# A 4096 x 4096 matmul by two levels of seven products: three first products in quarters, stores by row tile pairs, two more column pairs with kept sums

## The chip, the cores and the metric

The kernel runs on one core of one Trainium2 chip. The metric is the device time of one execution in microseconds. Three executions of the kernel before took 1523.41, 1525.5 and 1526.43 us, so the median is 1525.5 us.

A core has TensorE (PE, with its weight loads PEld), VectorE (DVE), ScalarE (ACT), GpSimd (POOL) and SyncE (SP). SP, ACT and POOL also issue transfers; each of the three has a queue of its own to the 16 DMA engines of the core.

## The reference

```python
def reference(a, b, alpha):          # a, b: 4096 x 4096 float32, alpha: 0.01
    x = np.matmul(a, b)
    return np.where(x > 0, x, alpha * x)
```

## The kernel before, in words

**Tiles.** The output is cut into regions of 1024 x 1024. Row groups g and column pairs j both run from 0 to 3. Region (0, 0) is done directly; the other fifteen stand in the list `regions` in this order: (0,1) (0,2) (0,3), then (1,2) (1,0) (1,3) (1,1), then (2,2) (2,0) (2,3) (2,1), then (3,2) (3,0) (3,1) (3,3). For a region, A is four blocks of 512 x 2048 (A11, A12, A21, A22) and B four blocks of 2048 x 512 (B11, B12, B21, B22), all in fp16 in SBUF. A block of B is two tiles (k = 0, 1) of 128 x 8 x 512.

**Outer level.** The eight block products are replaced by seven (`PRODUCTS`), over sums of A blocks (S1 to S4) and of B blocks (T1 to T4) that DVE makes: product 0 is A11 B11, product 1 is A12 B21, product 2 is S2 T2, product 3 is S3 T3, product 4 is S1 T1, product 5 is A22 T4 and product 6 is S4 B22. The T sums are made in place: T3 in the tiles of B12 and T2 in those of B11. In full, a product is 64 matmuls of 128 x 128 x 512 (line L831, `product`), into four PSUM banks, one for each row tile.

**Inner level.** Some products are themselves done by the same scheme, "in quarters": seven quarter products (`quarter_product`, L770) of 16 matmuls of 128 x 128 x 256, so 112 half-width matmuls in place of 64 full ones. Their operands are again sums: of quarters of a B block (`t3_of_b`, `sums_of_b`, on DVE) and of quarters of an A operand (`sums_of_a`). The sums of A are made once in the first region of a row group (those of S1 in the second), stored to DRAM (`kept_q`) and loaded again in each region by `load_sums` (L762), 512 KB each. In the kernel before, a region of groups 1 to 3 that is neither the first nor the last of its group, and (3,3), does products 3, 4, 5 and 6 in quarters (fourth, fifth, sixth and seventh in the code) and products 0, 1 and 2 in full. The first region of a group does its last two products in quarters; the last region of groups 1 and 2, which also brings in the next group's A ("turning"), does one.

**Order.** `manual_schedule` keeps each engine's instructions in the order in which the program writes them, and each engine works in that order. SP's queue thus holds, from the sixth product of a region to the start of the next region: stores of the V pair of outputs (`leave(v_pairs, 1, 1)`), loads of the next region's B21 (`fetch_b(i + 1, [(1, 0)])`, L544 where they come from `kept_half`), stores of the U2 pair (`leave(u2_pairs, 1, 0)`), then, behind the seventh product, loads of the next B22, the first half of S2 (`load_s2`, L789), and the stores of the last pair. ACT's queue carries the four sums for the seventh product. POOL's queue brings B from the input with a cast from fp32 (L547), two transfers of 512 KB for each tile.

**Buffers.** Three tiles of 16 KB a partition (`x_pool`) hold S1, S4 and, by turns, S2 and a tile `t` of four quarter sums. Three quarter-sized tiles (`a16_pool`) hold further sums and the rooms of the measures. Two output tiles for each of two sides (`c_pool`) are shared by U1, U2, V and the last pair; a tile is free again when its store has landed. `bank` sets alternate between regions: Y and Z are four PSUM banks each.

**Measures.** Every block of A and B is squared once on ACT (L231) and its column or row sums folded on DVE (L240 to L264) for a test of the input's range. Where a block is measured stands in `EARLY` and `MEASURED`.

**Kept data.** For column pair 2, T3 and T2 are stored in group 1 and loaded in groups 2 and 3 (`move_t`, L529). For pairs 0, 1 and 3 B21 and B22 are kept in fp16 (`kept_half`).

The two lines by which a PSUM bank of a first product becomes the start of the next sums (L1132) and a pair of outputs is stored (L1076) are

```python
        for mt in range(MT):
            nc.scalar.copy(z[mt], y[mt])
...
                for m in range(2):
                    nc.sync.dma_start(place(g, h, 2 * r + m, j, nt), t[:, m, :])
```

Of the kernel before, what the change touches and what calls it, by code (L numbers as in the profile page):

```python
# [37 lines left out]
OTHERS = (0, 3)  # L38

# [9 lines left out]
def kernel(  # L49
# [145 lines left out]
    def place(g, h, mt, j, nt):  # L195
        row = ((g * 2 + h) * MT + mt) * P
        col = (j * 2 + nt) * NT
        return out[row:row + P, col:col + NT]

# [314 lines left out]
    kept_t = {name: dram_pool.tile([2, P, KC * NT], DT, name=f"kept_{name}") for name in ("t3", "t2")}  # L514
# [12 lines left out]
    def move_t(name, t, k, out, queue=nc.sync):  # L527
        ends = kept_t[name][k], t.rearrange("p c n -> p (c n)")
        queue.dma_start(*(ends if out else ends[::-1]))  # L529

    def fetch_unit(i, u, nt, later=False):
# [7 lines left out]
        if g > 1 and j == CACHED and (half, nt) == (0, 1):  # L539
            move_t("t3", t, u, False)  # L540
# [89 lines left out]
    def judge(line):  # L630
# [29 lines left out]
        (1, 3): [B11], (2, 0): [B21], (2, 3): [B21], (2, 1): [B12], (3, 1): [B11, B21],  # L660
# [14 lines left out]
    kept_q = {name: dram_pool.tile([4, P, QUARTER], DT, name=f"kept_q{name}") for name in ("a22", "s4", "s1")}  # L675
    FIFTH = {(1, 0), (1, 3), (2, 0), (2, 3), (3, 0), (3, 1), (3, 3)}
# [123 lines left out]
    in_quarters = False  # L800
    for i, (g, j) in enumerate(regions):
# [6 lines left out]
        ybank = 0 if i % 2 == 0 else 4  # L808
        zbank = 4 - ybank
# [6 lines left out]
        def product(n, banks, first):  # L816
            name, half, nt = PRODUCTS[n]

# [3 lines left out]
            if n == 0 or n == 2 and in_fourth:  # L822
                order[-16:] = [(mt, k, c) for mt in range(MT) for k, c in todo[-4:]]
            elif n == 1 or n == 4 and in_fourth:
                order[:16] = [(mt, k, c) for mt in range(MT) for k, c in todo[:4]]
# [14 lines left out]

        def keep(banks, side):
            pairs, kept = new_c(side)
            for mt in range(MT):
                nc.scalar.copy(kept[mt], banks[mt])  # L844
            return pairs, kept

# [51 lines left out]
        def fifth_in_quarters(y, banks, tq, sx, pairs, between):  # L898
# [6 lines left out]
            onto = lambda r, n: [y[2 * r + m][:, n * HALF:(n + 1) * HALF] for m in range(2)]  # L905
# [6 lines left out]
            def more(r, n, room):  # L912
                for m, to in enumerate(onto(r, n)):
                    nc.vector.tensor_add(to, to, room[:, m])

            quarter_product(x[0, 1], b[1, 0], onto(0, 0))
            quarter_product(x[0, 0], b[0, 0], into(chain), True)
            one = copied(0, 0, chain)
            quarter_product(a_quarter(sx[4]), b[1, 1], onto(0, 1))
# [3 lines left out]
            quarter_product(x[1, 1], t(4), onto(1, 0))  # L923
# [9 lines left out]
            last = copied(1, 1, chain)  # L933
            for m in range(2):
# [3 lines left out]
        def sixth_in_quarters(pairs, banks, v_pairs, v, y, tq, sq):  # L938
# [20 lines left out]
            add(v, y)  # L959
# [28 lines left out]
        def seventh_in_quarters(y, one, other, tq, sq):  # L988
# [7 lines left out]
            onto = lambda r, n: [y[2 * r + m][:, n * HALF:(n + 1) * HALF] for m in range(2)]  # L996
            quarter_product(x[0, 1], b[1, 0], onto(0, 0))
# [3 lines left out]
            quarter_product(x[1, 1], t(4), onto(1, 0))  # L1001
# [8 lines left out]
            for mt in range(MT):  # L1010
                nc.vector.tensor_add(kept[mt], y[mt], kept[mt])
            return pairs

        def seventh_at_the_end(y, one, other, tq, sq, one_more):
# [9 lines left out]
            onto = lambda r, n: [part(y[2 * r + m], n) for m in range(2)]  # L1024
# [8 lines left out]
            for mt in (2, 3):  # L1033
                nc.scalar.copy(part(kept[mt], 1), part(y[mt], 1))
            quarter_product(x[0, 1], b[1, 0], onto(0, 0))
            for mt in range(2):
                more(mt, 0, part(y[mt], 0))
# [7 lines left out]
            quarter_product(sx(4), b[1, 1], onto(0, 1))  # L1045
            for mt in range(2):
                more(mt, 1, part(y[mt], 1))
# [7 lines left out]
            quarter_product(x[1, 1], t(4), onto(1, 0), by_row=True)  # L1055
            for mt in (2, 3):
                more(mt, 0, part(y[mt], 0))
# [12 lines left out]
        def leave(pairs, h, nt, some=(0, 1)):  # L1070
            for r, t in enumerate(pairs):
# [3 lines left out]
                for m in range(2):  # L1075
                    nc.sync.dma_start(place(g, h, 2 * r + m, j, nt), t[:, m, :])  # L1076
# [34 lines left out]
        y = [new_bank(ybank + mt) for mt in range(MT)]  # L1111
        z = [new_bank(zbank + mt) for mt in range(MT)]
# [6 lines left out]
        in_fifth = (g, j) in FIFTH  # L1119
        second_of_group = in_fourth and regions[i - 2][0] != g  # L1120
        early = [measure(i, *block) for block in EARLY.get((g, j), [])]
        for m in early[:1]:
# [3 lines left out]
        product(0, y, True)  # L1126
        if second_of_group:
            sums_of_s3(g, (2,))
        for m in early[:1]:
            m.end()  # L1130
        for mt in range(MT):
            nc.scalar.copy(z[mt], y[mt])  # L1132
        if second_of_group and g in [of for of, _ in FIFTH]:
            sums_of_a(g, "s1", new_a16)
        for m in early[1:]:
            m.begin()
        have_t2 = g > 1 and j == CACHED
        if have_t2:
            for k in ks:
                t = have_b[i, k, 0] = b_pool.tile([P, KC, NT], DT, name="b", tag="b11")  # L1140
                move_t("t2", t, k, False, nc.scalar)
        if middle:
            middle.begin()
        for k in ks:
            if have_t2:
                break
# [9 lines left out]
        for m in early[1:]:  # L1156
# [6 lines left out]
        note_rows()  # L1163
        if first_of_group:
# [35 lines left out]
        if in_fifth:  # L1200
# [8 lines left out]
        if in_fifth:  # L1209
# [265 lines left out]
```

## Time and profile before

| | before |
|---|---|
| median of three executions | 1525.5 us |
| profiled execution, its own time | 1526.13 us |
| its span, first to last instruction | 1524.2 us |
| mean granted TensorE clock | 0.999 |
| PE busy | 1512.9 us (99%) |
| DVE busy | 1166.7 us (77%) |
| ACT busy | 512.2 us (34%) |
| POOL busy | 258.3 us (17%) |
| DMA, mean over the span | 244 GB/s |
| moved on SP's queue | 232.95 MB |
| moved on POOL's queue | 112.22 MB |
| moved on ACT's queue | 25.56 MB |

Busy PE is a modelled number: matmuls are pipelined, so a share of 99% says that PE hardly waited, not that each matmul ran at its peak. Times in the views are microseconds from the start of the span. "L831" is line 831 of the kernel. A row of the engines' timeline is a start, a duration to the last end, and a group of like instructions; in square brackets stands how long the engine was idle ahead of it and what it then waited for. A row of DMA issues gives the queue, the count, the size of one transfer and the median time from its issue to its landing.

### The profile page before, as it was taken

The numbers are of one execution on the slowest core, as the hardware profiler recorded it, in microseconds if no ns is written. First come the engines' busy times: TensorE is split into PE (matmuls) and PEld (weight loads), VectorE is DVE, ScalarE is ACT, GpSimd is POOL, SyncE is SP. The second block draws the span as 40 slices with busy tenths as digits, with TensorE's granted clock in tenths as the row PEclk, the third lists the DMA queues.
The fourth block names the chain that finished last, engine by engine and source line by source line (L and its number), as shares of the span: only waits on it lengthen the run. The fifth ranks groups of instructions, "written<-read, shape, count | busy, mean of one in ns | idle before, by whom it ended". The sixth has DMA issues, their size and how long they took to land.

```text
span 1524.2 us, 22803 instructions
## 1 busy us (share of the span) xinstructions
PE 1512.9 (99%) x9003; PEld 879.2 (58%) x9003; DVE 1166.7 (77%) x1221; ACT 512.2 (34%) x885; POOL 258.3 (17%) x426
## 2 busy tenths in 40 slices
PE   9999999999999999999999999999999999999998
PEld 4444444444446577584544748667554475848667
DVE  4588867666896597777779598777978779888797
ACT  2411535537410123124661132323574113252221
POOL 5641110233202011012320101000331100101000
PEclk9999999999999999999999999999999999999999
DMA  9999995999889999999898968859999894968935
GB/s 247 189 215 206 242 285 164 174 187 193 235 330 247 285 300 288 290 289 271 199 273 317 287 252 187 312 151 330 220 239 313 223 337 148 276 238 205 331 122 172
DMA packets 197767, 372.29 MB, mean 244 GB/s; under 512 B 19345, under 2 KB 132241, under 8 KB 184594
## 3 DMA queue, kind: packets, MB, share of 16 engines
q0 software_dynamic: 119808, 112.22, 46.7%
q1 hardware_dynamic: 71218, 232.95, 41.0%
q10 hardware_dynamic: 6624, 25.56, 4.3%
q8 instruction: 72, 1.18, 0.3%
q14 instruction: 45, 0.37, 0.1%
HBM read 359.66 MB, written 121.11 MB: 315 GB/s over the span
## 4 chain that ended last, share of the span: by engine, by line
PE 58%; DMA 6%; DVE 1%; issue 1%; SPq 0%; POOL 0%; DVEq 0%; POOLq 0%
PE ps L831 34%; PE ps L770 25%; DMA b<-in_b_dram 5%; DMA q<-kept_qs 1%; DVE b L603 0%; DVE c L313 0%; DVE c L1028 0%; POOL b L547 0%; SPq L1076 0%; DVE b L696 0%; DVE b L1225 0%; SPq L762 0%; DVEq L603 0%; DVEq L313 0%; POOLq L547 0%
## 5 line engine op out<-in xcount | busy, mean ns | idle before, releaser
L831 PE MATMUL ps<-b,a 128*128 128x512 f16 x2624 | 570.6, 379 | 0.0
L831 PEld LDWEIGHTS <-a 128*128 128x128 f16 x2624 | 256.7, 98 | 307.8
L831 PE MATMUL ps<-b,s 128*128 128x512 f16 x1792 | 391.3, 379 | 0.0
L831 PEld LDWEIGHTS <-s 128*128 128x128 f16 x1792 | 175.4, 98 | 210.9
L603 DVE TENSOR_TENSOR b<-b 128x4096 f16<-128x4096 f16 x97 | 218.9, 2286 | 51.3 <-DMA b<-in_b_dram 33.1
L547 POOL DMA_DIRECT2D b<-in_b_dram x128 | 94.8, 745 | 870.5 <-PE ps L770 266.1
L770 PEld LDWEIGHTS <-q 128*128 128x128 f16 x1872 | 182.6, 98 | 23.2 <-DMA q<-kept_qs 1.6
L844 ACT COPY c<-ps 128x512 f32<-128x512 f32 x164 | 85.9, 596 | 287.5 <-PE ps L831 277.7
L133 POOL DMA_DIRECT2D a<-in_a_dram x252 | 137.5, 553 | 246.5 <-ACT junk L622 81.3
L142 DVE STREAM_TRANSPOSE a<-a 128x512 uint32<-128x512 uint32 (+2 forms) x120 | 127.0, 1107 | 66.5 <-DMA a<-in_a_dram 66.5
L313 DVE SCALAR_TENSOR_TENSOR c<-c 128x1024 f32<-128x1024 f32 (+2 forms) x123 | 141.9, 1196 | 17.7 <-ACT c L844 17.4
L622 ACT ACTIVATE junk<-a 128x512 bf16<-128x512 f16 x192 | 121.2, 631 | 72.8 <-DMA a<-in_a_dram 67.7
L770 PEld LDWEIGHTS <-a 128*128 128x128 f16 x1200 | 117.4, 98 | 14.7
L231 ACT ACTIVATE sq<-b 128x2048 bf16<-128x2048 f16 x60 | 111.3, 1911 | 43.1 <-DVE sq L240 36.7
L770 PE MATMUL ps<-b,q 128*128 128x256 f16 x1008 | 118.6, 273 | 0.0
L283 PE MATMUL ps<-b,a 128*128 128x512 f16 x512 | 112.2, 379 | 0.5 <-ACT a L380 0.2
L770 PEld LDWEIGHTS <-s 128*128 128x128 f16 x960 | 93.8, 98 | 14.2 <-DVE b L603 1.3
L770 PE MATMUL ps<-q,q 128*128 128x256 f16 x864 | 99.9, 273 | 0.9 <-DMA q<-kept_qs 0.9
L770 PE MATMUL ps<-b,a 128*128 128x256 f16 x752 | 88.3, 273 | 0.0
L283 PEld LDWEIGHTS <-a 128*128 128x128 f16 x512 | 49.7, 98 | 60.8 <-issue 1.4
L1132 ACT COPY ps<-ps 128x512 f32<-128x512 f32 x60 | 32.8, 572 | 147.8 <-PE ps L831 147.8
L1063 DVE TENSOR_TENSOR c<-ps,c 128x512 f32<-128x512 f32 x72 | 44.6, 683 | 47.6 <-PE ps L831 38.0
(125 smaller groups left out, 1053.6 us busy)
## 6 DMA issues: line engine op xcount, KB each, us to landing
b<-in_b_dram POOLq DMA_DIRECT2D x136, 512.0 KB, 12.4
out_dram<-c SPq DMA_DIRECT2D x240, 256.0 KB, 7.8
a<-in_a_dram POOLq DMA_DIRECT2D x244, 128.0 KB, 5.7
b<-kept_half SPq DMA_DIRECT2D x28, 1024.0 KB, 11.8
b<-kept SPq DMA_DIRECT2D x20, 1024.0 KB, 9.2
q<-kept_qs ACTq DMA_DIRECT2D x40, 512.0 KB, 7.2
s<-kept_s SPq DMA_DIRECT2D x18, 1024.0 KB, 9.1
q<-kept_qs SPq DMA_DIRECT2D x28, 512.0 KB, 6.1
```

Source lines behind the costliest of these rows:

```text
L133: nc.gpsimd.dma_start(a16[32 * q:32 * q + 32], src.rearrange("(g i) w -> i g w", i=32))
L142: nc.vector.transpose(part.rearrange("p c m e -> p c (m e)").bitcast(U32) .rearrange("p c (g i) -> p g c i", i=32), src[:, :, i * n:(i + 1 ...
L231: nc.scalar.activation(to, self.parts[n], SQUARE)
L283: nc.tensor.matmul(ps, a_cols(at[0, h, u], c, mt, (h, u) == (0, 0)), bt[0, u, nt][:, c, :], start=first, stop=last,)
L313: nc.vector.scalar_tensor_tensor(t, t, alpha, t, op0=MULT, op1=MAX if alpha <= 1 else MIN)
L547: nc.gpsimd.dma_start(t[:, c:c + 4, :], b_rows(j, u, c, 4, nt, g > 0))
L603: nc.vector.tensor_tensor(f(to), f(x0), f(x1), op)
L622: nc.scalar.activation(junk, piece[:, q, :], SQUARE, accum_out=to[:, 4 * n + q:4 * n + q + 1])
L770: nc.tensor.matmul(to[m], xq[:, c // 2, rows, c % 2], yq[:, c, :], start=first and c == 0 and m < banks, stop=c == KC - 1, skip_group_chec ...
L831: nc.tensor.matmul(banks[mt], a_cols(t, c, mt, t is first_a), B(half, nt, k)[:, c, :], start=first and (k, c) == todo[0], stop=(k, c) == t ...
L844: nc.scalar.copy(kept[mt], banks[mt])
L1063: nc.vector.tensor_add(to, bank, to)
```

## The change

Six things are done.

1. In the regions (2,3), (3,1) and (3,3) (`FIRST`) product 0 is done in quarters too, by `first_in_quarters`. Its banks are laid out by quarters (one bank holds 256 rows by 256 columns as two halves), so products 1 and 2 of these regions use half-width matmuls as well, 128 in place of 64. The Y and Z banks rotate in another way there.
2. The operands are made ahead by `for_the_first`, a generator that the seventh product of the region before steps through: three sums of B11 quarters on DVE and four loads of A11 sums on SP's queue. The A11 sums are made and stored in the first regions of groups 2 and 3. S2 is loaded only after the first product.
3. Outputs leave in one transfer for two row tiles (`places`).
4. T3 and T2 of pairs 0 and 3 are stored in group 2 and loaded in group 3 (`KEPT_T`).
5. The measure of B21 of pair 0 moves from (2,0) to (3,0), that of B11 of pair 1 from (3,1) to (1,1). In the three regions the early measure is done after the first product.
6. The path for regions without a fifth product in quarters goes; no region of before took it.

```diff
+KEPT_T = {CACHED: 1, 0: 2, 3: 2}
...
-    kept_t = {name: dram_pool.tile([2, P, KC * NT], DT, name=f"kept_{name}") for name in ("t3", "t2")}
+    kept_t = {(name, j): dram_pool.tile([2, P, KC * NT], DT, name=f"kept_{name}_{j}")
+              for name in ("t3", "t2") for j in KEPT_T}
...
-        if g > 1 and j == CACHED and (half, nt) == (0, 1):
-            move_t("t3", t, u, False)
+        if g > KEPT_T.get(j, G) and (half, nt) == (0, 1):
+            move_t("t3", j, t, u, False)
...
-        (1, 3): [B11], (2, 0): [B21], (2, 3): [B21], (2, 1): [B12], (3, 1): [B11, B21],
+        (1, 3): [B11], (1, 1): [B11], (2, 3): [B21], (2, 1): [B12], (3, 0): [B21], (3, 1): [B21],
...
-    FIFTH = {(1, 0), (1, 3), (2, 0), (2, 3), (3, 0), (3, 1), (3, 3)}
+    FIRST = {(2, 3), (3, 1), (3, 3)}
...
+        in_first = (g, j) in FIRST
+        if in_first:
+            shared_bank = Z[1]
+            Y, Z = [Z[2], Z[3], Y[0], Z[0]], [Y[1], Y[2], Z[1], Y[3]]
+        else:
+            Y, Z = Z, Y
...
             name, half, nt = PRODUCTS[n]
+            if in_first:
+                for k in ks:
+                    for q in (0, 1, 3, 2):
+                        for c in range(KC):
+                            for m, to in enumerate(into(banks[q])):
+                                nc.tensor.matmul(
+                                    to, a_cols(operand(g, name, k), c, q // 2 * 2 + m),
+                                    B(half, nt, k)[:, c, q % 2 * HALF:(q % 2 + 1) * HALF],
+                                    start=False, stop=(k, c) == (ks[-1], KC - 1), skip_group_check=True,
+                                )
+                return
...
-        def seventh_in_quarters(y, one, other, tq, sq):
+        def seventh_in_quarters(y, one, other, tq, sq, between):
...
-            quarter_product(sx(4), b[1, 1], onto(0, 1))
-            quarter_product(x[1, 1], t(4), onto(1, 0))
+            quarter_product(sx(4), b[1, 1], onto(y, 0, 1))
+            next(between)
+            quarter_product(x[1, 1], t(4), onto(y, 1, 0))
+            next(between)
             quarter_product(sx(2), t(2), into(one))
             nc.scalar.copy(block(0, 1), pair(one))
+            next(between)
             quarter_product(sx(1), t(1), into(other), True)
+            next(between)
             nc.vector.tensor_add(block(0, 1), pair(other), block(0, 1))
             quarter_product(sx(3), b[0, 1], into(one))
+            next(between)
...
+        def for_the_first(tq, sq, first_t, first_s):
+            y1 = quarters_of_b(i + 1, 0, 0)
+            tt = nc.vector.tensor_tensor
+            f = lambda n: b_quarter(first_t[n])
+            first_s[1] = new_a16()
+            load_sums("a11", first_s, (1,))
+            yield
+            first_s[2] = tq[4]
+            load_sums("a11", first_s, (2,))
+            yield
+            first_t[3], first_t[2] = new_a16(), tq[2]
+            tt(f(3), y1[1, 1], y1[0, 1], SUB)
+            tt(f(2), f(3), y1[0, 0], ADD)
+            yield
+            first_t[1], first_s[3] = new_a16(), tq[1]
+            tt(f(1), y1[1, 1], f(2), SUB)
+            load_sums("a11", first_s, (3,))
+            yield
+            first_s[4] = sq[3]
+            load_sums("a11", first_s, (4,))
+            yield
+
+        def first_in_quarters(y, shared, z, tq, sq):
+            room = new_c(side)[0][1][:, :, :HALF]
+            b = quarters_of_b(i, 0, 0)
+            x = quarters_of_a(g, "a11")
+            one, other, third, chain = y
+            t = lambda n: b_quarter(tq[n])
+            sx = lambda n: a_quarter(sq[n])
+            quarter_product(x[0, 0], b[0, 0], into(chain), True)
+            nc.scalar.copy(one, chain)
+            quarter_product(sx(1), t(1), into(shared), True)
+            nc.scalar.copy(room, pair(shared))
+            tq[4] = new_a16()
+            nc.vector.tensor_tensor(t(4), b[1, 0], t(2), SUB)
+            quarter_product(sx(2), t(2), into(chain))
+            nc.scalar.copy(other, chain)
+            quarter_product(x[0, 1], b[1, 0], into(one))
+            nc.scalar.copy(z[0], one)
+            quarter_product(sx(3), t(3), into(chain))
+            nc.scalar.copy(third, chain)
+            nc.vector.tensor_add(pair(chain), pair(chain), room)
+            quarter_product(sx(4), b[1, 1], into(other))
+            nc.vector.tensor_add(pair(other), pair(other), room)
+            quarter_product(x[1, 1], t(4), into(third))
+            z[2] = new_bank(Z[2])
+            for to, bank in ((3, chain), (1, other), (2, third)):
+                nc.scalar.copy(z[to], bank)
...
-                for m in range(2):
-                    nc.sync.dma_start(place(g, h, 2 * r + m, j, nt), t[:, m, :])
+                nc.sync.dma_start(places(g, h, 2 * r, j, nt), t)
...
-        product(0, y, True)
+        if in_first:
+            shared = new_bank(shared_bank)
+            first_in_quarters(y, shared, z, first_t, first_s)
+            new_s(g, "s2")
+            load_s2(g, ks[0])
+        else:
+            product(0, y, True)
...
-        have_t2 = g > 1 and j == CACHED
+        have_t2 = g > KEPT_T.get(j, G)
...
-            if g == 1 and j == CACHED:
-                move_t("t3", B(0, 1, k), k, True)
-                move_t("t2", B(0, 0, k), k, True)
+            if g == KEPT_T.get(j):
+                move_t("t3", j, B(0, 1, k), k, True)
+                move_t("t2", j, B(0, 0, k), k, True)
...
+        if a11_sums:
+            sums_of_a(g, "a11", new_a16, (1, 2, 3), made)
         if first_of_group:
             sum_a(g, "s3")
             if g:
                 sum_a(g, "s4")
+        if a11_sums:
+            sums_of_a(g, "a11", new_a16, (4,), made)
...
-                kept_c = seventh_in_quarters(*rest)
+                first_t, first_s = {}, {}
+                between = for_the_first(tq, sq, first_t, first_s) if next_first else nothing()
+                kept_c = seventh_in_quarters(*rest, between)
                 fetch_b(i + 1, [(1, 1)], (1, 0))
-                new_s(g, "s2")
-                load_s2(g, 1)
+                if not next_first:
+                    new_s(g, "s2")
+                    load_s2(g, 1)
                 leave(kept_c, 0, 1)
```

More of the change, by code (lines that the diff above doesn't have):

```diff
@@ L933, in fifth_in_quarters @@
             last = copied(1, 1, chain)
+            if in_first:
+                more(1, 0, last)
+                more(1, 1, last)
+                return
             for m in range(2):
@@ L1009, in seventh_in_quarters, with nothing @@
             nc.vector.tensor_add(block(1, 1), pair(other), block(1, 1))
-            for mt in range(MT):
-                nc.vector.tensor_add(kept[mt], y[mt], kept[mt])
-            return pairs
+            add_pieces(pairs, y)
+            return pairs
+        def nothing():
+            while True:
+                yield
[19 more added lines that the diff above has]
+            load_sums("a11", first_s, (4,))
+            yield
@@ L1023, in seventh_at_the_end @@
             part = lambda t, n: t[:, n * HALF:(n + 1) * HALF]
-            onto = lambda r, n: [part(y[2 * r + m], n) for m in range(2)]
+            of_y = lambda mt, n: onto(y, mt // 2, n)[mt % 2]
             ones = [part(bank, 0) for bank in (one, one_more)]
@@ L1109, in bring_a @@
                     turn_a_in(h, half, n)
-        y = [new_bank(ybank + mt) for mt in range(MT)]
-        z = [new_bank(zbank + mt) for mt in range(MT)]
+        y = [new_bank(Y[mt]) for mt in range(MT)]
+        z = [None if in_first and mt == 2 else new_bank(Z[mt]) for mt in range(MT)]
         middle, late_ones, fifth, sixth = MEASURED.get((g, j), (None, [], None, None))
@@ L1118 @@
         in_fourth = in_quarters and not first_of_group
-        in_fifth = (g, j) in FIFTH
+        next_first = not final and regions[i + 1] in FIRST
         second_of_group = in_fourth and regions[i - 2][0] != g
         early = [measure(i, *block) for block in EARLY.get((g, j), [])]
-        for m in early[:1]:
+        at_once, afterwards = ([], early) if in_first else (early[:1], early[1:])
+        for m in at_once:
             m.begin()
@@ L1238 @@
             keep_x21(g, "a22")
-        z = [new_bank(zbank + mt) for mt in range(MT)]
+        z = [new_bank(Z[mt]) for mt in range(MT)]
         def s3_fourth(room):
@@ L1303 @@
             if turning:
-                z = [new_bank(zbank + mt) for mt in range(MT)]
+                z = [new_bank(Z[mt]) for mt in range(MT)]
                 for mt in range(MT):
```

152 lines of the change are left out of this document (80 added, 72 removed).

## The prediction

> **What bounds the kernel now.** I read the page's first lines, then who waited on PE, then the chain that ended last.
>
> ```profile
> span 1524.2 us, 22803 instructions
> ...
> PE 1512.9 (99%) x9003; PEld 879.2 (58%) x9003; DVE 1166.7 (77%) x1221; ACT 512.2 (34%) x885; POOL 258.3 (17%) x426
> ```
> ```profile
> PE ps L770 <- DMA q<-kept_qs: 0.9, 1, 0.9
> PE ps L770 <- DVE b L1225: 0.6, 2, 0.3
> PE ps L770 <- DVE b L603: 0.6, 1, 0.6
> ```
> ```profile
> 632.97 11.27 DMA q<-kept_qs
> ...
> 644.28 43.84 PE ps L770 x400
> ...
> 918.19 48.91 PE ps L770 x448
> 967.10 41.44 PE ps L831 x192
> ```
>
> From 644 us to the tail the chain is PE alone: TensorE bounds the kernel, and after the start its waits come to 2.1 us, all before 645. Removed matmuls are therefore worth their full time, and any transfer that comes late to PE costs its full time. The one wait on a transfer is a warning: a load of quarter sums on SP's queue took 11.27 us to land and PE stood for it.
>
> The chain also gives PE's pace. A full matmul takes 41.44 / 192 = 0.2158 us, a half-width one 48.91 / 448 = 0.1092 us, so a quarter product of 16 takes 1.75 us. The half-width pace already holds the weight load of each.
>
> **The change part by part.** *PE's work.* A first product falls from 64 x 0.2158 = 13.81 us to 112 x 0.1092 = 12.23, a gain of 1.58. Products 1 and 2 of the same region become 128 half-width matmuls each, 13.98 in place of 13.81, a loss of 0.17 each. The net is 1.25 us for a region and 3.7 us for three. That is the whole gain the change can have on PE's own work.
>
> *The loads of the A11 sums.* Four loads of 512 KB are put on SP's queue inside the seventh product. The second quarter product of the new first product needs the first of them. Its room is that of the seventh product's first used sum, free after the third quarter product. I look at the boundary from (2,0) to (2,3): PE's rows, SP's rows, then each transfer's time to landing (asked for one at a time; 955.20, 963.39, 966.64).
>
> ```profile
> 958.20 1.91 PE L770 MATMUL ps<-b,q 128*128 128x256 f16 x16
> 959.95 1.91 PE L770 MATMUL ps<-q,s 128*128 128x256 f16 x16
> ...
> 966.93 27.79 PE L831 MATMUL ps<-b,a 128*128 128x512 f16 x128
> ```
> ```profile
> 955.20 0.33 SPq L544 DMA_DIRECT2D b<-kept_half  x1
> 958.59 5.12 SPq L1076 DMA_DIRECT2D out_dram<-c  x4
> 963.39 0.33 SPq L1076 DMA_DIRECT2D out_dram<-c  x1
> 966.64 0.33 SPq L544 DMA_DIRECT2D b<-kept_half  x1
> ```
> ```profile
> b<-kept_half SPq DMA_DIRECT2D x1, 1024.0 KB, 14.7
> out_dram<-c SPq DMA_DIRECT2D x1, 256.0 KB, 10.1
> b<-kept_half SPq DMA_DIRECT2D x1, 1024.0 KB, 9.3
> ```
> ```profile
> 960.00:975.00 15.00, 15.00 (x104) 9.91 (x102) 7.84 (x10) 7.80 (x7) 0.00 (x0) 1.00 1.08 371
> ```
>
> The room is free at 959.95 + about 0.2, and SP can issue the load then or, with its wait for the U2 stores, a few us later. When it issues hardly matters. The window's last column but one says that the DMA engines are full (a share of 1.08), and SP's transfers land in the order in which they were issued: the B21 load of 955.20 at 969.9, the last U2 store at 963.39 + 10.1 = 973.5, the next 1 MB at 966.64 + 9.3 = 975.9. The new load stands between the last two. It is half as large as the 1 MB that took 2.4 us behind the store, so it lands at 973.5 + 1.2 = 974.7. PE wants it one quarter product into the region, at 966.93 + 1.75 = 968.68. PE waits 6.0 us. The other three loads follow at 1.2 us each, faster than PE's 1.75 for a quarter product, and cost nothing more. All this traffic (B21, U2, V, B by POOL) is there in the changed kernel too; stores in pairs move the same bytes.
>
> ```profile
> 1332.76 0.33 SPq L1076 DMA_DIRECT2D out_dram<-c  x1
> 1336.07 0.33 SPq L544 DMA_DIRECT2D b<-kept_half  x1
> 1336.25 4.05 PE L831 MATMUL ps<-b,a 128*128 128x512 f16 x18
> ...
> 1423.01 0.33 SPq L1076 DMA_DIRECT2D out_dram<-c  x1
> 1426.60 3.62 PE L831 MATMUL ps<-b,a 128*128 128x512 f16 x16
> ```
> ```profile
> out_dram<-c SPq DMA_DIRECT2D x1, 256.0 KB, 10.5
> b<-kept_half SPq DMA_DIRECT2D x1, 1024.0 KB, 9.6
> out_dram<-c SPq DMA_DIRECT2D x1, 256.0 KB, 10.8
> ```
>
> In the same way at (3,1): last store landed at 1343.3, next 1 MB at 1345.7, so the load at 1344.5 against a need at 1336.25 + 1.75 = 1338.0: 6.5 us. At (3,3) it would be 1433.8 + 1.2 = 1435.0 against 1428.35, 6.7 us, but there something goes:
>
> ```profile
> q0 software_dynamic: 119808, 112.22, 46.7%
> q1 hardware_dynamic: 71218, 232.95, 41.0%
> ```
>
> POOL's transfers (q0) cost 0.467 x 1524.2 / 112.22 = 6.3 us of all 16 engines for a MB, SP's (q1) 2.7. B12 of (3,3), 2.1 MB, now comes as T3 on SP's queue: 13.3 us becomes 5.6. B12's transfers stand ahead of this boundary, so do the 7.7 us saved, and the load lands about when it is wanted. I take 0 and keep 0 to 6.7.
>
> *What a wait of 6 us does to PE's pace.* The rows nearest to it are the first matmuls of all and those after the 0.9 us wait.
>
> ```profile
> 1.19 4.75 PE L106 MATMUL wp<-w 128*128 128x512 f16 x11 [1.19 <-DVE x L92]
> ...
> 644.28 0.94 PE L770 MATMUL ps<-q,q 128*128 128x256 f16 x7 [0.87 <-DMA q<-kept_qs]
> ```
>
> The first eleven started 0.42 us apart, twice the pace, so 11 x 0.21 = 2.3 us were lost to a cold start. After the short wait seven half-width matmuls took 0.94, which is full pace. Six us lies between; I take half, 1.15 us for each wait, 2.3 for two, with ends 0 and 2.3 each. The Trainium skill, "TensorE: Matmul & The Clock Gate", Part 1, has a rule that speaks against the change here: the clock falls to half after an idle window of about 3.4 us and returns after a busy one. By it each wait would cost another 1.7 us, and the sum below would be 1.1 us higher; no wait in this trace is long enough to show it.
>
> *DVE and ACT.* The new first product's three B sums fall in the end of the seventh product, where DVE has time (7.84 us busy of 15 in the window above); the fourth and the two bank additions stand where the whole early measure was. B sums of (3,0) and (3,3), four of 6.82 / 3 = 2.3 us each, go. (3,0) gets a measure instead (DVE's rows there in before):
>
> ```profile
> 1260.09 1.23 DVE L719 TENSOR_TENSOR q<-s,q 128x2048 f16<-128x2048 f16 x1 [3.35 <-DMA kept_qs<-q]
> ...
> 1263.61 6.82 DVE L603 TENSOR_TENSOR b<-b 128x4096 f16<-128x4096 f16 x3
> 1270.35 1.22 DVE L240 TENSOR_TENSOR sq<-sq 128x2048 bf16<-128x2048 bf16 x1
> ...
> 1277.45 2.35 DVE L313 SCALAR_TENSOR_TENSOR c<-c 128x1024 f32<-128x1024 f32 x2
> 1279.72 6.69 DVE L603 TENSOR_TENSOR b<-b 128x4096 f16<-128x4096 f16 x3
> ```
> ```profile
> 1287.35 2.89 PE L770 MATMUL ps<-b,s 128*128 128x256 f16 x25
> ```
>
> A measure holds DVE 1277.45 - 1270.35 = 7.1 us, less than the 9.2 removed, but the second measure's squares on ACT now wait for rooms that the S1 sums' stores free. The T1 sum ends at 1286.4 for a product that starts at 1287.35: cover 0.9 us. I take 0, ends 0 and 2. The measure in (1,1) is like that of (2,1), where PE never waited: 0. The A11 sums (four of 1.23 us, as the L719 row, and 2 MB of stores) delay DVE in (2,2) and (3,2) ahead of a stage with room:
>
> ```profile
> 838.50:852.30 13.80, 13.80 (x66) 6.33 (x65) 2.97 (x4) 1.43 (x3) 2.96 (x4) 1.00 1.23 216
> ```
>
> DVE is busy 2.97 of 13.8 us there. I take 0, ends 0 and 3 for both groups, if a store that frees a sum's room is late. *Kept T3 and T2.* The 4 MB of stores in (2,0) go where the DMA share is low, those in (2,3) and the T2 loads (ACT's queue) have product 1's 14 us ahead of them: 0. S2's later load also has product 1 in front of it: 0. *Stores in pairs.* Half the issues on SP. The gain is at most the 0.9 us wait at 644, which hangs on a full queue, so I take 0.
>
> **Sum.** -3.7 + 6.0 + 6.5 + 2.3 = +11.1 us. The profiled execution took 1526.13, so 1537.2 against it. The median of the runs shown is 0.6 lower, and so is my forecast: 1536.6 us.
>
> **The rivals.** *The loads are not held up (faster).* The place is the second quarter product of the three regions. The page gives loads of this kind on SP a median of
>
> ```profile
> q<-kept_qs SPq DMA_DIRECT2D x28, 512.0 KB, 6.1
> ```
>
> and 960.2 + 6.1 = 966.3 is ahead of 968.68. It decides at 8.5 us from issue to landing. Then only -3.7 is left: 1521.8. Against it: that median comes mostly from loads in slack stages, and the transfers that SP issued around this place took 9.3 to 14.7 us. Within this rival a smaller wait is late next: the ACT copy into a c tile needs the U2 stores landed (973.5), 0.7 us behind PE's own order at (2,3) and 1.2 at (3,1); with it the time is 1523.7, no measurable change.
>
> *All three wait.* If T3 in place of B12 doesn't relieve (3,3), add 6.7 and 1.15: 1544.5. For it: T3's 2 MB join the very queue that the load stands in. Against it: the 7.7 us.
>
> *DVE at (3,0) or in the first regions becomes late*, with the ends 2 and 3 above: up to 1541.6. The clock's full price on two waits, 2 x 1.15 more, gives 1538.9.
>
> **How the numbers follow.** Two waits of 4 to 8 us (with DVE's and the clock's ends, 1529 to 1543): 0.70. All three wait: 0.08. Loads in time, 1521.8: 0.15. Loads in time but the c tile late, or waits about as large as the gain, around 1525: 0.07. The measurement can tell about 0.2%, 3 us, so faster is the third case (0.15), same the fourth (0.07) and slower the first two (0.78). The range 1523 to 1546 leaves out most of the third case and little else; the likeliest case's own range is 1529 to 1543.
>
> **What the profile of after would show.** PE's waits list: a wait on q<-kept_qa at L770 of about 6 us, twice, in the second quarter product of (2,3) and (3,1), and none or a short one at (3,3). In the chain, a DMA piece q<-kept_qa ahead of the first product's matmuls, with SP's loads of it taking 10 to 15 us to landing. A full-width count lower by 3 x 192 matmuls and a half-width one higher by 3 x 368 at the same pace. A granted clock a little under 0.999 if the cold start comes back. I would be wrong if those loads land within 8.5 us of their issue, or if the queue is emptier there than before.

## The result, and the profile after

The changed kernel takes 1544.41 us (median of five executions, 1542.68 to 1548.55) against 1525.5 before (the median of five as well; the three times named above are the lowest, the middle and the highest). The ratio worked out from all runs is 1.0127, 95% interval 1.0116 to 1.0139. The kernel is slower, by some 19 us. Its profiled execution took 1542.68 us itself, 16.55 more than that of before, with a span of 1540.9 us and a mean granted clock of 0.993.

The page's first lines, after:

```profile
span 1540.9 us, 23717 instructions
...
PE 1514.1 (98%) x9531; PEld 933.4 (61%) x9531; DVE 1175.1 (76%) x1227; ACT 519.4 (34%) x897; POOL 252.2 (16%) x418
```

PE is busy for 1.2 us more in a span that is 16.7 longer, so it stood still for most of the rest. Who made it wait most, in the list of PE's waits (sum, count, longest, in us):

```profile
PE ps L777 <- DMA q<-kept_qa: 11.3, 2, 6.1
PE ps L777 <- DVE b L610: 4.8, 1, 4.8
```

Two waits on loads of A11 sums, and one on DVE. The places, in PE's timeline: the second quarter products of (2,3), (3,1) and (3,3), each after the first one of 1.91 us, and then product 4 of (3,0), S1 T1, the first that is done in quarters there.

```profile
966.19 1.91 PE L777 MATMUL ps<-b,a 128*128 128x256 f16 x16
974.24 3.45 PE L777 MATMUL ps<-q,q 128*128 128x256 f16 x16 [6.13 <-DMA q<-kept_qa]
```
```profile
1348.77 1.91 PE L777 MATMUL ps<-b,a 128*128 128x256 f16 x16
1355.82 3.60 PE L777 MATMUL ps<-q,q 128*128 128x256 f16 x16 [5.14 <-DMA q<-kept_qa]
1359.21 2.16 PE L777 MATMUL ps<-q 128*128 128x256 f16 x16
```
```profile
1445.05 1.91 PE L777 MATMUL ps<-b,a 128*128 128x256 f16 x16
1446.79 1.91 PE L777 MATMUL ps<-q,q 128*128 128x256 f16 x16
```
```profile
1298.19 5.34 PE L777 MATMUL ps<-b,s 128*128 128x256 f16 x32 [4.85 <-DVE b L610]
```

A group of 16 half-width matmuls lasts 1.91 us at full pace and one of 32 lasts 3.66. After each of the three waits the matmuls run slower for a while: 3.45 - 1.91 = 1.54 us are lost at (2,3), 1.69 and 0.25 (two groups, less the overlap of their ends some 1.9 together) at (3,1), and 5.34 - 3.66 = 1.68 at (3,0).

Why the load is late at (2,3) stands on SP's queue. The first load of an A11 sum is issued at 959.47 and lands 14.7 us later, at 974.2; at (3,1), issued at 1342.05, it takes 13.7.

```profile
959.47 7.24 SPq L769 DMA_DIRECT2D q<-kept_qa  x4
```
```profile
q<-kept_qa SPq DMA_DIRECT2D x1, 512.0 KB, 14.7
q<-kept_qa SPq DMA_DIRECT2D x1, 512.0 KB, 13.7
```

Why DVE is late at (3,0) takes three engines' rows. ACT's queue, then ACT itself, then DVE, then SP's queue, all in (3,0), then the time to landing of three of the four stores of S1 sums, and what the queues of ACT (q10) and SP (q1) moved from 1267 to 1273 us (packets, MB, share of the 16 engines):

```profile
1266.26 0.37 ACTq L536 DMA_DIRECT2D b<-kept_t  x1
...
1277.92 7.31 ACT L237 ACTIVATE sq<-b 128x2048 bf16<-128x2048 f16 x4 [11.32 <-DMA kept_qs<-q]
```
```profile
1258.96 1.22 DVE L246 TENSOR_TENSOR sq<-sq 128x2048 bf16<-128x2048 bf16 x1
...
1275.58 1.22 DVE L726 TENSOR_TENSOR q<-s,q 128x2048 f16<-128x2048 f16 x1 [5.90 <-DMA kept_qs<-q]
...
1281.66 1.23 DVE L246 TENSOR_TENSOR sq<-sq 128x2048 bf16<-128x2048 bf16 x1 [4.85 <-ACT sq L237]
...
1291.44 6.69 DVE L610 TENSOR_TENSOR b<-b 128x4096 f16<-128x4096 f16 x3
```
```profile
1267.31 9.84 SPq L727 DMA_DIRECT2D kept_qs<-q  x4
```
```profile
kept_qs<-q SPq DMA_DIRECT2D x3, 512.0 KB, 8.8
```
```profile
q10 hardware_dynamic: 236, 1.80, 91.8%
q1 hardware_dynamic: 21, 0.09, 3.5%
```

T2 is now loaded here, 2 MB on ACT's queue, at the moment when SP stores the S1 sums. The three stores take 8.8 us in the median. A store frees the room of its sum, and the next S1 sum on DVE (5.90 us idle) and the squares of a measure on ACT (11.32 us) wait for such rooms. This is the second measure of (3,0), that of B22, which stood here in the kernel before too. The moved measure is the first: its rows on DVE begin at 1258.96 and stand ahead of the S1 sums, so they put the sums and their stores back, into the time of T2's loads. DVE then waits for the squares of B22, and its next three B sums, two for T4 and the first of T1, run until 1298, when PE has been waiting for 4.85 us.

### The profile page after: what moved, and what is told of

Read it like the earlier page. It is cut to its first block, busy times and chain, and to the rows that moved or that the text cites. A ratio compares the mean times of both kernels' runs of the same rounds, so it can differ in the third digit from the quotient of the medians.

```text
span 1540.9 us, 23717 instructions
## 1 busy us (share of the span) xinstructions
PE 1514.1 (98%) x9531; PEld 933.4 (61%) x9531; DVE 1175.1 (76%) x1227; ACT 519.4 (34%) x897; POOL 252.2 (16%) x418
## 3 DMA queue, kind: packets, MB, share of 16 engines
q8 instruction: 76, 1.25, 0.3%
## 5 line engine op out<-in xcount | busy, mean ns | idle before, releaser
L854 PE MATMUL ps<-b,a 128*128 128x512 f16 x2240 | 487.2, 379 | 0.0
L854 PEld LDWEIGHTS <-a 128*128 128x128 f16 x2240 | 219.2, 98 | 263.0
L854 PE MATMUL ps<-b,s 128*128 128x512 f16 x1600 | 349.4, 379 | 0.0
L854 PEld LDWEIGHTS <-s 128*128 128x128 f16 x1600 | 156.6, 98 | 188.3
L610 DVE TENSOR_TENSOR b<-b 128x4096 f16<-128x4096 f16 x89 | 200.7, 2285 | 40.5 <-DMA b<-in_b_dram 34.2
L777 PEld LDWEIGHTS <-q 128*128 128x128 f16 x2064 | 203.1, 99 | 37.7 <-DMA q<-kept_qa 11.8
L777 PEld LDWEIGHTS <-a 128*128 128x128 f16 x1344 | 131.5, 98 | 16.3
L777 PE MATMUL ps<-q,q 128*128 128x256 f16 x960 | 114.6, 277 | 11.4 <-DMA q<-kept_qa 11.3
L289 PE MATMUL ps<-b,a 128*128 128x512 f16 x512 | 112.2, 379 | 0.5 <-ACT a L386 0.2
L777 PEld LDWEIGHTS <-s 128*128 128x128 f16 x960 | 94.6, 99 | 19.5 <-DVE b L610 6.6
L777 PE MATMUL ps<-b,a 128*128 128x256 f16 x848 | 99.8, 273 | 0.0
L289 PEld LDWEIGHTS <-a 128*128 128x128 f16 x512 | 49.7, 98 | 60.8 <-issue 1.4
L777 PE MATMUL ps<-b,s 128*128 128x256 f16 x544 | 64.2, 277 | 6.0 <-DVE b L610 4.8
L1243 ACT COPY ps<-ps 128x512 f32<-128x512 f32 x48 | 26.4, 572 | 123.6 <-PE ps L854 123.6
## 6 DMA issues: line engine op xcount, KB each, us to landing
b<-kept_half SPq DMA_DIRECT2D x28, 1024.0 KB, 13.7
```

What stands on the lines that cost most here:

```text
L289: nc.tensor.matmul(ps, a_cols(at[0, h, u], c, mt, (h, u) == (0, 0)), bt[0, u, nt][:, c, :], start=first, stop=last,)
L610: nc.vector.tensor_tensor(f(to), f(x0), f(x1), op)
L777: nc.tensor.matmul(to[m], xq[:, c // 2, rows, c % 2], yq[:, c, :], start=first and c == 0 and m < banks, stop=c == KC - 1, skip_group_chec ...
L854: nc.tensor.matmul(banks[mt], a_cols(t, c, mt, t is first_a), B(half, nt, k)[:, c, :], start=first and (k, c) == todo[0], stop=(k, c) == t ...
```

## Experiments

The theory was that three things cost the time, each by itself: the load behind a full SP queue at the second quarter product, PE's slow matmuls after such waits, and, in (3,0), stores of the S1 sums held up by T2's loads together with the measure moved there. The rival for the first was that the loads are late because of the quarters' own work (rooms that come free too late), for the last that the measure alone is too much for DVE.

| run | edit | median us | ratio to before, 95% |
|---|---|---|---|
| after | | 1544.41 | 1.0127 (1.0116 to 1.0139) |
| e1 | no first product in quarters | 1530.87 | 1.0032 (1.0019 to 1.0044) |
| e2 | A11 loads on ACT's queue | 1542.06 | 1.0102 (1.0085 to 1.0120) |
| e3 | B21 load moved behind the seventh product | 1532.33 | 1.0045 (1.0028 to 1.0062) |
| e4 | measure back in (2,0) | 1539.07 | 1.0093 (1.0076 to 1.0110) |
| e5 | T2 of (3,0) on SP's queue | 1538.31 | 1.0081 (1.0066 to 1.0096) |
| e6 | e3 and e4 | 1526.55 | 1.0004 (0.9995 to 1.0013) |
| e7 | before, with stores in pairs | 1525.86 | 0.9998 (0.9988 to 1.0007) |
| e8 | e1 and e4 | 1524.80 | 0.9991 (0.9982 to 1.0001) |
| e9 | e6, first load ahead of the U2 stores | 1524.42 | 0.9992 (0.9983 to 1.0002) |
| e10 | e9, without (3,3) | 1524.04 | 0.9988 (0.9979 to 0.9997) |

**e1: no first product in quarters.**

```diff
-    FIRST = {(2, 3), (3, 1), (3, 3)}
+    FIRST = set()
```

> The three first products go back to full ones; all else stays as after. If the waits of 6.3 and 5.3 us in front of the second quarter product, each with some 1.8 us of half clock behind it, come from the new loads, they go (15.2 us) and the 3.7 us gained on TensorE go too: 1544.4 - 15.2 + 3.7 = 1533 us, with only the wait on the T1 sum in (3,0) (5.0 us and 1.7 us of half clock) left of the large ones. If instead the extra traffic of the kept T3 and T2 is what makes transfers late, long waits on transfers stay and the time is 1540 us or more.

Measured 1530.87. PE's waits, e1:

```profile
PE ps L777 <- DVE b L610: 4.5, 2, 4.2
```

All waits on A11 sums are gone with the quarters, and 13.5 us with them. The wait in (3,0) stays at 4.2 us. It thus does not need the first products, and what is left over before, 1530.87 - 1525.5 = 5.4 us, is about that wait and the slow matmuls behind it.

**e2: the A11 loads on ACT's queue,** ahead of which little stands.

```diff
-            load_sums("a11", first_s, (1,))
+            load_sums("a11", first_s, (1,), nc.scalar)
...
-            load_sums("a11", first_s, (4,))
+            load_sums("a11", first_s, (4,), nc.scalar)
```

(and the two loads between them alike)

> The four loads of A11 sums are issued from ScalarE's queue, in the same places. If they were late because they stood behind B21 and the U2 stores in one queue, the first lands 6 to 8 us after about 960 instead of 10 to 14, and TensorE no longer waits for it; but the loads then take engine time from the U2 stores, which land some 3 us later, and the copy into the c tile that those stores free waits for them: a wait of 2 to 4 us two quarter products later, for ScalarE. Time 1533 to 1540 us. If instead the engines are simply full and the queue makes no difference, the first load lands as late as in after and the time stays at 1544 us.

A miss: 1542.06, only 2 us better. PE's waits, then ACT's timeline, then PE's, all e2:

```profile
PE ps L777 <- DVE b L610: 6.7, 2, 4.9
PE ps L777 <- ACT c L1048: 6.0, 2, 3.2
```
```profile
961.38 7.24 ACTq L769 DMA_DIRECT2D q<-kept_qa  x2
968.65 0.59 ACT L1048 COPY c<-ps 128x512 f32<-128x512 f32 x1 [8.44 <-DMA b<-kept_half]
```
```profile
969.29 3.57 PE L777 MATMUL ps<-b,q 128*128 128x256 f16 x16 [2.71 <-ACT c L1048]
...
974.45 1.91 PE L777 MATMUL ps<-q,q 128*128 128x256 f16 x16
```

The mechanism for the load held: it landed 9.0 us after its issue, and the second quarter product starts at 974.45 without a wait. But the wait moved to ACT. Two loads, issued over 7.24 us, kept ACT from copying a bank of the seventh product, and PE waited for that bank, 2.71 us here and 3.2 at the other place, with slow matmuls again. The profile puts ACT's stop to the landing of B21, which the second load does not read. In the trace the transfers of SP and ACT take eight semaphores by turns. The semaphore of the second load was last that of the B21 load issued at 952.64, which landed 15.6 us later, at 968.2; the second load was issued at 968.29. So the issue stood on an engine that also copies, and the cost was the copy.

**e3: the load of the next B21 moved behind the seventh product,** in front of the regions with a first product in quarters.

```diff
-            fetch_b(i + 1, [(1, 0)], (1, 0) if in_quarters else ks)
+            if not next_first:
+                fetch_b(i + 1, [(1, 0)], (1, 0) if in_quarters else ks)
...
+                if next_first:
+                    fetch_b(i + 1, [(1, 0)], (1, 0))
```

> Only the order on SyncE's queue changes: the 2 MB of the next B21 are issued behind the seventh product, so behind the four loads, in front of (2,3), (3,1) and (3,3). By the queue theory the loads land some 5 us earlier: the first at about 969 to 970, a wait of 0 to 1.5 us in place of 6.3 and 5.3, and no half clock. B21 lands at about 978, ahead of product 1. Time 1544.4 - 15.2 plus at most 3 = 1529 to 1532 us. If the bytes ahead in the queue are not the cause, the waits stay and the time is 1544 us; if B21 becomes late instead, a wait of some us stands in front of product 1.

Measured 1532.33, 12.1 us better than the changed kernel. PE's waits, and the first load's landing, e3:

```profile
PE ps L777 <- DVE b L610: 6.1, 2, 5.3
PE ps L777 <- DMA q<-kept_qa: 1.0, 1, 1.0
```
```profile
q<-kept_qa SPq DMA_DIRECT2D x1, 512.0 KB, 9.5
```

Only what is ahead in the queue was changed; the load's own issue (959.54), room and size are as they were. It lands after 9.5 us in place of 14.7, and the two waits shrink to one of 1.0 us. That settles the first point against the rooms: the loads were late because of the megabytes in front of them. The wait in (3,0), 5.3 us, is untouched.

**e4: the measure of B21 of pair 0 back in (2,0).**

```diff
-        (1, 3): [B11], (1, 1): [B11], (2, 3): [B21], (2, 1): [B12], (3, 0): [B21], (3, 1): [B21],
+        (1, 3): [B11], (1, 1): [B11], (2, 0): [B21], (2, 3): [B21], (2, 1): [B12], (3, 1): [B21],
```

> The measure of B21 of pair 0 goes back from (3,0) to (2,0). If the two measures in (3,0) make the T1 sum late (VectorE waits for the squares, which wait for rooms that the S1 sums' stores free), the wait of 5.0 us and the 1.7 us of half clock in (3,0) go: 1544.4 - 6.7 = 1537.7 us. If it is the loads of T2 that hold the stores up whatever is measured, the wait stays, perhaps 2 us shorter, and the time is 1542 us or more.

**e5: T2 of (3,0) on SP's queue,** behind the stores of the S1 sums, with the measure left where the change put it.

```diff
-                move_t("t2", j, t, k, False, nc.scalar)
+                move_t("t2", j, t, k, False, nc.sync if (g, j) == (3, 0) else nc.scalar)
```

> Both measures stay in (3,0); only the two 1 MB loads of its T2 go from ScalarE's queue to SyncE's, where they stand behind the four stores of S1 sums. If these loads hold the stores up (in after the first three landed 8 to 9.5 us after their issue, once T2 had landed), the stores land within 3 to 4 us, the squares of the second measure start some 4 to 6 us earlier, and the wait of 5.0 us in (3,0) falls to 0 to 1 us with no half clock behind it: 1544.4 - 6 = 1538 us. If the two measures alone fill VectorE and ScalarE, the wait stays near 5 us and the time at 1544 us.

Measured 1539.07 and 1538.31: both take 5 to 6 us off. PE's waits of e4, then of e5, then the issues of e4's S1 stores, then the landing of e5's S1 stores and its squares in (3,0):

```profile
PE ps L777 <- DMA q<-kept_qa: 12.1, 2, 6.1
PE ps L777 <- DVE b L610: 1.2, 1, 1.2
```
```profile
PE ps L777 <- DMA q<-kept_qa: 11.9, 2, 6.0
PE ps L777 <- DVE b L610: 1.0, 1, 1.0
```
```profile
1260.20 6.61 SPq L727 DMA_DIRECT2D kept_qs<-q  x4
```
```profile
kept_qs<-q SPq DMA_DIRECT2D x4, 512.0 KB, 2.7
```
```profile
1271.99 7.32 ACT L237 ACTIVATE sq<-b 128x2048 bf16<-128x2048 f16 x4 [4.75 <-DVE s L795]
```

Either one cures (3,0): the waits on DVE that are left, 1.2 and 1.0 us, lie in group 1, at 547 us, where the kernel before waits too (0.6 us). So the measure alone does not make DVE late (e5 keeps it), and T2's loads on ACT's queue alone do not (e4 keeps them): it takes the two together. Without the moved measure (e4) the first S1 store is issued at 1260.20 in place of 1267.31, and three of the four are issued ahead of T2's loads, of which the first comes at 1265.83. The first two land in 4.9 us; the fourth takes 9.2, and T1 is made in time all the same. With T2 off the second queue (e5) the stores land in 2.7 us in place of 8.8 and the squares start some 6 us earlier. The Trainium skill, "DMA: Bandwidth & Descriptors", "Queues, rings and completion order", says that each DMA engine takes turns between the queues that have work for it; by that a store on one queue slows when megabytes come on another. The stores of the changed kernel agree in direction, but not in amount: from 1267 to 1273 us T2's queue moved 236 packets and SP's 21. Why the stores got so few is not shown.

**e6: e3 and e4 together.**

> The new B21 order and the measure back in (2,0) together. If the waits are independent, 1532.3 (B21 later alone) less the 5.3 us that the measure's move back gained alone (1544.4 to 1539.1) gives 1527 us; if the remaining wait in (3,0) was longer there (5.4 us and 2.6 of half clock in its profile), 8 us go and the time is 1524.4 us, 0.1% below before. The 3.7 us of saved matmuls would then be seen against before, less 1 to 2 us of short waits on the first load. If taking away these waits opens another, 1530 us or more.

Measured 1526.55. The single gains add up: 12.1 of e3 and 5.3 of e4 make 17.4, and e6 is 17.9 us below the changed kernel. PE's waits, e6, and one of DVE's last additions:

```profile
PE ps L777 <- DMA q<-kept_qa: 2.7, 2, 1.5
PE ps L835 <- DMA s<-kept_s: 0.4, 1, 0.4
```
```profile
1516.51 0.43 DVE L1132 TENSOR_TENSOR c<-ps,c 128x256 f32<-128x256 f32 x1 [0.65 <-PE ps L777]
```

3.1 us of waits are still there in the regions with a first product in quarters, about what the fewer matmuls save. Short waits in group 1 come beside them, as in the kernel before. At the end of (3,3) DVE stands 0.65 us for PE: with banks laid out by quarters, both row halves of the last quarter product lie in one bank, and the addition of the first half waits for the second too. The same wait, 0.65 us, is in the changed kernel. In the kernel before the addition followed without one, and so it does in e10, where (3,3) has its full first product. The row of the kernel before:

```profile
1516.57 0.42 DVE L1028 TENSOR_TENSOR c<-ps,c 128x256 f32<-128x256 f32 x1
```

**e7: the kernel before with stores in pairs only.**

```diff
-                for m in range(2):
-                    nc.sync.dma_start(place(g, h, 2 * r + m, j, nt), t[:, m, :])
+                nc.sync.dma_start(places(g, h, 2 * r, j, nt), t)
```

> The kernel before with nothing but the stores of two row tiles in one transfer. If the wait of 0.9 us at 644 us hangs on the number of issues on SyncE, and the end of the kernel on the last stores, up to 1.5 us go: 1524 us. If all hangs on bytes, nothing changes: 1525.6 us.

Measured 1525.86, ratio 0.9998: half the issues of stores on SP are worth nothing here. The 0.9 us wait that a shorter queue might have taken away stays, at 0.7.

**e8: no first products in quarters, and the measure back (e1 and e4).**

> Full first products and the measure back in (2,0): what is left of the change is the stores in pairs, the kept T3 and T2 of pairs 0 and 3 and one measure moved to (1,1). By my prediction these cost nothing and gain nothing: 1525.6 us, as before. If the kept T3 and T2 (12 MB more traffic, 8 of it stores) cost time on their own, 1528 us or more; if less cast traffic by GpSimd's queue helps, 1523 us.

Measured 1524.80, ratio 0.9991 (0.9982 to 1.0001). All that the change does beside the first products and that measure, kept T3 and T2 included, moves the time by no more than 0.2%. The A11 sums are not made in this run, so it says nothing of them.

**e9: e6 with the first A11 load issued ahead of the two U2 stores.**

```diff
             load_sums("a11", first_s, (1,))
+            leave(u2_pairs, 1, 0, do=(False, True))
...
-        leave(u2_pairs, 1, 0)
+        leave(u2_pairs, 1, 0, do=(True, not next_first))
```

(`do` says which half of `leave` is done: the leaky function, the store)

> As the kernel with B21 later and the measure back, and the first A11 load is also issued ahead of the two U2 stores (1 MB). In that kernel the first load landed at 969.6, 4.3 us behind the landing of the first U2 store; without the stores in front it should land near 967, ahead of its need at 968, and U2 near 970, ahead of the c tile's copy. The waits of 1.6 and 1.4 us in front of the second quarter product go: 1526.55 - 3.0 = 1523.5 us, 0.15% below before. If SyncE's queue order was not what set them, 1526.5 us.

**e10: e9 without (3,3).**

```diff
-    FIRST = {(2, 3), (3, 1), (3, 3)}
+    FIRST = {(2, 3), (3, 1)}
```

> The same with the first product of (3,3) in full. In the last region the layout by quarters puts the two row halves of the last quarter product in one bank, and VectorE's last additions wait for all of it (0.65 us of idle that before does not have); with the full product that wait goes, and so does the S2 wait of 0.6 us, against 1.25 us of matmuls more. 1523.5 + 1.25 - 0.8 - 0.6 = 1523.4 us, the same as its neighbour. If the last region's gain is whole, 1524.7 us.

Measured 1524.42 and 1524.04. In e9 the first load lands 6.6 us after its issue and the largest wait on A11 sums is 0.4 us, now in the third quarter product. First the landing and PE's waits of e9, then PE's waits of e10:

```profile
q<-kept_qa SPq DMA_DIRECT2D x1, 512.0 KB, 6.6
```
```profile
PE ps L777 <- DMA q<-kept_qa: 0.7, 2, 0.4
```
```profile
PE ps L777 <- DVE b L610: 1.8, 1, 1.8
PE ps L854 <- DVE b L610: 0.9, 1, 0.9
```

Both beat the changed kernel by 20 us and stand within 0.2% of the kernel before. Against e8, which has no first product in quarters, the gain is 0.4 us in e9 and 0.8 in e10, where 3 x 1.25 and 2 x 1.25 would be the matmuls' worth. Measured against its own round's kernel before, e9 gains nothing on e8 (0.9992 and 0.9991) and e10 some 0.5 us. The measurement does not resolve that difference. Part of it went to e9's small waits and to the tail; e10's 1.8 and 0.9 us lie in group 1, which the edit does not touch, and the rest stays open.

## Why the prediction was right, and where it was off

The forecast was 1537.2 us against the profiled execution and 1536.6 against the median. The profiled execution took 1542.68 and the median is 1544.41. The side came out, and so did the place and the mechanism of the two forecast waits; the sum was short by 5.5 us in the profiled execution, and by 7.8 in the median, which lies 1.7 us above the profiled execution. The median lies in the stated range, 1523 to 1546, but above the range of the case held likeliest, 1529 to 1543. It falls on the 1544.5 of the rival by which all three regions wait, and that is chance: (3,3) did not wait. What filled the gap is the other rival, DVE late at (3,0), with some 6.5 us where 2 had been kept for it. That the time still fell in the stated range is owed to the range's width.

- **PE's work, -3.7: right.** The profile counts 4416 full matmuls of products before and 3840 after (the groups below), 576 = 3 x 192 fewer, and 528 more matmuls in all, so 1104 = 3 x 368 more of half width. 448 of them take 49.02 us in the chain after, 48.91 before. The groups of full products, before, then after, and a piece of the chain, after:

```profile
L831 PE MATMUL ps<-b,a 128*128 128x512 f16 x2624 | 570.6, 379 | 0.0
L831 PE MATMUL ps<-b,s 128*128 128x512 f16 x1792 | 391.3, 379 | 0.0
```
```profile
L854 PE MATMUL ps<-b,a 128*128 128x512 f16 x2240 | 487.2, 379 | 0.0
...
L854 PE MATMUL ps<-b,s 128*128 128x512 f16 x1600 | 349.4, 379 | 0.0
```
```profile
1485.38 49.02 PE ps L777 x448
```

- **The wait at (2,3), +6.0: right.** 6.13, with the load landed at 974.2 where 974.7 was worked out from the stores and megabytes ahead of it. e3 and e9, which change what stands ahead, showed that it is those.
- **The wait at (3,1), +6.5: a little high.** 5.14; the load took 13.7 us and landed at 1355.8. In e4 and e5, where (3,0) is not late, this wait is 6.02.
- **(3,3), 0: right,** no wait at all, but only just: the load was issued at 1438.32 and took 8.0 us, so it landed at 1446.3, 0.5 us before the second quarter product began. That T3 in place of B12 is the reason was not tested by itself.
- **The cold matmuls, +1.15 each: too low.** They cost 1.54 and 1.9. The half-way value between the ends was a choice without a row. The estimate from the rule of the Trainium skill, "TensorE: Matmul & The Clock Gate", Part 1, was 1.7, and the changed kernel's trace agrees with that size; other runs lost 1.3 to 2.9 (last section).
- **DVE and ACT in (3,0), 0: the term that failed.** It measured 4.85 us of wait and 1.7 of slow matmuls. The step saw that "the second measure's squares on ACT now wait for rooms that the S1 sums' stores free", with a cover of 0.9 us. It weighed the measure's 7.1 us on DVE against the 9.2 that go, and not the order: the moved measure stands ahead of the S1 sums, the sums that go stood behind them, so the S1 stores come 7.1 us later. It also took these stores at their speed in the kernel before. A few sentences on, T2's loads were put on ACT's queue at that same time and costed at nothing, because PE has product 1's 14 us ahead of them. That cover is right for their own landing, and is no cover for what they delay: the stores beside them take 8.8 us, against 5.6 in the kernel before and 2.7 in e5, without these loads. The end of 2 us kept for it was too near for the same reason.
- **The measure in (1,1), the kept T sums' stores, the A11 sums in (2,2) and (3,2), stores in pairs, 0: right** as far as PE's waits tell. e7 and e8 bound all of these but the A11 sums at 0.2% of the time.
- **Not foreseen:** the 0.65 us in the tail, from the banks' new layout.

With these the differences are -3.7 + 6.1 + 5.1 + 1.5 + 1.9 + 4.85 + 1.7 = +17.5 us, and +18.1 with the tail. The last instruction of DVE ends 17.9 us later than before (1536.2 against 1518.2). The spans differ by 16.7, because from there to the end it took 4.7 us in place of 6.0; that stretch holds the last stores and takes 4.0 to 6.3 us in the other profiles.

The rival by which the loads land after about 6 us, the median of their kind on the page, fell: they took 13.7 and 14.7. At (3,3) the load took 8.0, and e9 shows that with the queue in another order the rival would have held at (2,3) too, at 6.6 us.

## What to carry to other kernels

A load's time to landing is read from the transfers that stand ahead of it on its queue at that moment, not from the median of its kind; when a step adds a small load with a near deadline, move the large loads with later deadlines behind it. When a step adds a transfer that is itself in no hurry, look up what else is under way at that time on the other queues, and who waits for the buffers that those transfers free. When work moves, look at what it stands ahead of, not only at the sum of busy time: here 7.1 us for 9.2 made an engine late. And a saving of fewer matmuls is worth its time only as long as every wait that it brings stays shorter than it: here 1.25 us a region against waits of 5 to 6.

## What the runs showed of the hardware

**How long a stop slows PE.** After waits of 2.71 us (e2), 4.85, 5.14 and 6.13 us (after) the half-width matmuls took 1.5 to 1.9 us longer. Over all runs the loss was 1.3 us (e4 and e5, after 5.9 to 6.1) to 2.9 (e2 at (3,0), after 4.86, and e4 at (3,1), after 6.02). After waits of 1.46 us (e6) and 1.81 us (e10) nothing was lost:

```profile
969.68 1.92 PE L777 MATMUL ps<-q,q 128*128 128x256 f16 x16 [1.46 <-DMA q<-kept_qa]
```
```profile
549.56 1.92 PE L777 MATMUL ps<-b,s 128*128 128x256 f16 x16 [1.81 <-DVE b L610]
```

So the point lies between 1.8 and 2.7 us in these runs, which is below the idle window of about 3.4 us that the same page of the Trainium skill gives.

The granted clock shows why like waits cost unlike amounts. A row of a stretch gives its bounds, its length, the busy time of PE, PEld, DVE, ACT and POOL (with the number of instructions), the granted clock, the DMA engines' share and GB/s. After at (2,3), then e4 at (3,1):

```profile
970.60:977.40 6.80, 3.16 (x15) 2.24 (x16) 1.96 (x2) 0.00 (x0) 0.00 (x0) 0.50 1.04 422
```
```profile
1349.30:1356.00 6.70, 5.86 (x28) 4.20 (x29) 1.23 (x1) 0.59 (x1) 0.00 (x0) 0.50 1.03 429
```

The clock was half for 6.8 us at both places, and for 3.4 us in (3,0) of the changed kernel; between its start and its end no run shows another length. PE loses half of what it works in that time: at (2,3) it still waited for more than half of it and lost 1.5 us of 3.16, in e4 the low clock began late in the wait and PE lost 2.9 of 5.86.

**An issue that waits for another queue's transfer.** In e2 ACT stood some 7 us at the issue of a load (961.38 to 968.29 with the issue before it), until a transfer of SP had landed whose data it did not need but whose semaphore it took over.
